# A two-layer hybrid decoder step: gate weights in 48 columns, norm vectors by rows, and head 0's projections dealt out between the small tokens' blocks of w_in

## The chip, the core and the metric

The kernel runs on one core of a Trainium2 chip. Its time is the device time of one execution, the median of several runs in microseconds (us). The core has five engines that work side by side, each in its own fixed order: TensorE (PE, matrix products into PSUM), VectorE (DVE), ScalarE (ACT), GpSimd (POOL), and SyncE (SP), which here only issues DMA transfers between the device's memory (HBM) and on-chip memory (SBUF). An engine that waits for something holds up all that stands behind it on that engine.

## The reference

One inference step of two layers, each followed by a squared-ReLU MLP and a layer norm. The first layer is gated linear attention (GLA), the second differential attention over a paged cache; the change lies in the first. Its input is a prompt of 1024 tokens, 16 meta tokens ahead of it, and 8 decode sequences with one new token each, every one with a stored state per head. In float32:

```python
h = x @ w_in                                    # 1024 -> q, k (4 heads x 128), v, r (4 x 256), g_low (16)
q, k, v, r, g_low = jnp.split(h, ...)
lg = log_sigmoid(g_low @ w_gate + b_gate) / 16  # one log decay per token, head and key column
b = cumsum(lg)                                  # within a chunk
o = (q * exp(b)) @ state + sum_j(q_i * k_j * exp(b_i - b_j)) v_j
new_state = exp(b_last) * state + (k * exp(b_last - b)).T @ v
out = (rms_norm(o, g_norm) * silu(r)) @ w_out   # then residual, layer norm with ln_mix_g, ln_mix_b
```

The outputs are both token sets after the two layers, the final GLA state of the prompt, the updated states of the 8 decode sequences, and the new rows of the cache.

## The kernel before

Products over the prompt are made exact enough for float32 by three products of a rounded type: an operand is split into a high and a low part, and `mm3` (L194 to L197) issues high x high, low x high and high x low. Weights are loaded as `raw` (L180) and split by ScalarE (L182) and GpSimd (L183). The prompt is transposed by TensorE (L264) and split (L191, L192) into XH and XL, in two halves `c` of 512 tokens.

The first layer runs in these steps, as the code is written:

- The meta and decode tokens, 24 rows called the small tokens, are multiplied with all of `w_in`. That streams in blocks of 1 MB through two buffers `swt`: eight blocks for q, k and v (L223, matmuls L280) and four for r (L229, L285).
- Their gate, scores and output follow in a chain across TensorE, ScalarE and VectorE: g_low (L324), transposes of q and k (L329), the gate product (L338), the transposed keys (L368), the meta tokens' state (L376, copied by ScalarE at L377), the scores (L385, L394), the product with v (L405).
- The 8 decode states, 512 KB each, pass through three buffers: load (L410), product (L413), the new k v term on GpSimd (L414), update on VectorE (L416), store (L417). The load of sequence `b + 3` waits for the store of sequence `b`.
- g_low of the prompt for both halves (L560), 16 columns of the array wide, three products for each of 8 blocks of the inner dimension.
- For each of four heads: q and k of both halves (matmuls at L195 to L197, 96 in all, copied to `gq` and `gk`, two buffers each), v of both halves (192 matmuls). Then for each half the gate product (L602), `log_gate` (ScalarE L314 to L316, VectorE L318 and L319), the running sum (L607), scores by a hierarchy of levels (VectorE L351, L356, L357; TensorE L617, L632), a transpose (L652), and outputs and state (L660 to L662).

PSUM is handed out by three pools: three banks `mmt` for the large products, three `axt` for transposes, gate products, scores and outputs, and `smt` for the small tokens.

The order on each engine is not that of the code. A scheduler places the instructions in a simulated timeline, by the order of the code as priority and by when operands and buffers are free; so work of head 1 can stand between steps of head 0. On SyncE a transfer also waits until an earlier one of its semaphore has landed.

## Time and profile before

| | us |
|---|---|
| median of 3 runs (lowest, highest) | 2921.35 (2921.29, 2924.93) |
| the profiled execution | 2915.81 |
| its span | 2914.1 |
| TensorE busy in the span | 2783.9 (96%) |
| VectorE, GpSimd, ScalarE busy | 1857.9, 1145.4, 1038.3 |
| mean granted TensorE clock | 0.978 |
| start of head 1's first gate product (L602) | 188.54 |

The page gives each engine's busy time over the whole span, an average over stages that are limited by different things. For a change in the first layer it is better to look at stretches of time there, at the waits of TensorE with what ended each, and at the rows of the engine that it waited for. The granted clock is the share of full speed that TensorE had. "L413 x24" counts records: a float32 product that isn't split leaves two.

### The profile page before, as it was taken

To read this page: it belongs to the slowest core of one execution; us is meant where nothing else is said; L and a number is where in the kernel's file an instruction comes from. 1 tells how busy PE (TensorE), PEld (TensorE's weight loads), DVE (VectorE), ACT (ScalarE), POOL (GpSimd) and SP (SyncE) were. 2 spreads that over 40 slices of the span, in tenths; PEclk is the share of its full clock that TensorE was granted. 3 is DMA by queue.
4 is the path that set the end of the run, shared out by engine and by line. 5 is a ranking of instruction groups with operands and counts; after the bars stand their busy time and mean duration, and the time that the engine had idled before them with its cause. 6 is when DMAs were issued, how large, how long until landed. Compare 5 with 4: busy or idle time off the path is not lost. (4 is left out here: it accounts for less than half of the span.)

```text
span 2914.1 us, 52192 instructions
## 1 busy us (share of the span) xinstructions
PE 2783.9 (96%) x19668; PEld 2275.1 (78%) x19668; DVE 1857.9 (64%) x2976; ACT 1038.3 (36%) x2071; POOL 1145.4 (39%) x885
## 2 busy tenths in 40 slices
PE   8999999999999999999989999989898999999996
PEld 5776668987777777777888986878788889797985
DVE  2664544458877877777676731878438755838378
ACT  2343354151122122122411111777325535345343
POOL 1321122234333333433323430122326766677666
PEclk9999999999999999999999998999899999999998
DMA  8667541524798888988488988463427878796972
GB/s 262 210 214 248 187 168 39 191 73 164 255 341 309 309 328 310 331 315 321 137 274 288 360 298 260 102 135 84 116 98 214 230 224 234 195 288 163 270 205 86
DMA packets 299308, 643.83 MB, mean 221 GB/s; under 512 B 35168, under 2 KB 150880, under 8 KB 287792
## 3 DMA queue, kind: packets, MB, share of 16 engines
q1 hardware_dynamic: 267520, 531.15, 52.8%
q0 software_dynamic: 31536, 109.35, 15.2%
q8 instruction: 155, 2.54, 0.3%
q14 instruction: 97, 0.79, 0.1%
HBM read 582.89 MB, written 40.91 MB: 214 GB/s over the span
## 5 line engine op out<-in xcount | busy, mean ns | idle before, releaser
L183 POOL TENSOR_TENSOR wlo<-raw,whi 128x512 fp32r<-128x512 f32 x256 | 361.2, 1425 | 786.0 <-ACT whi L182 697.6
L195 PE MATMUL mmt<-whi,XH 128*128 128x256 f32 (+1 forms) x1824 | 554.0, 305 | 7.5 <-DVE qr L1051 3.8
L196 PE MATMUL mmt<-wlo,XH 128*128 128x256 f32 (+1 forms) x1824 | 550.8, 303 | 0.5 <-POOL wlo L183 0.5
L195 PE MATMUL mmt<-XH,whi 128*128 128x512 f32 (+1 forms) x1376 | 480.1, 350 | 15.7 <-DVE HL L192 6.4
L197 PE MATMUL mmt<-XH,wlo 128*128 128x512 f32 (+1 forms) x1376 | 479.4, 350 | 0.0
L197 PE MATMUL mmt<-whi,XL 128*128 128x256 f32 x1536 | 440.5, 287 | 6.8 <-DVE XL L192 6.8
L195 PEld LDWEIGHTS mmt<-whi,XH 128*128 128x128 f32 x1824 | 346.3, 190 | 43.6 <-issue 19.8
L182 ACT CAST whi<-raw 128x512 fp32r<-128x512 f32 x256 | 152.4, 619 | 619.0 <-PE mmt L197 247.3
L196 PEld LDWEIGHTS mmt<-wlo,XH 128*128 128x128 f32 x1824 | 346.6, 190 | 25.0 <-issue 11.7
L771 DVE TENSOR_REDUCE sc<-pg 128x16 f32<-128x1024 f32 x256 | 309.6, 1214 | 78.4 <-POOL pg L770 74.9
L197 PEld LDWEIGHTS mmt<-whi,XL 128*128 128x128 f32 x1536 | 292.3, 190 | 22.7 <-issue 14.8
L196 PE MATMUL mmt<-XL,whi 128*128 128x512 f32 x768 | 307.6, 400 | 0.0
L195 PEld LDWEIGHTS mmt<-XH,whi 128*128 128x128 f32 x1376 | 261.2, 190 | 57.5 <-DVE HL L192 8.2
L770 DVE TENSOR_TENSOR pg<-pg,qb 128x1024 f32<-128x1024 f32 x192 | 261.3, 1366 | 59.1 <-DMA pg<-in_cache_k 42.9
L197 PEld LDWEIGHTS mmt<-XH,wlo 128*128 128x128 f32 x1376 | 261.2, 190 | 43.6 <-issue 12.0
L770 POOL TENSOR_TENSOR pg<-pg,qb 128x1024 f32<-128x1024 f32 x64 | 156.3, 2443 | 286.3 <-DMA pg<-in_cache_k 215.0
L195 PE MATMUL mmt<-whi,HH 128*128 128x512 f32 x512 | 205.3, 401 | 1.4 <-DVE Y L995 1.4
L196 PE MATMUL mmt<-wlo,HH 128*128 128x512 f32 x512 | 204.5, 399 | 0.0
L197 PE MATMUL mmt<-whi,HL 128*128 128x512 f32 x512 | 203.7, 398 | 0.0
L196 PEld LDWEIGHTS mmt<-XL,whi 128*128 128x128 f32 x768 | 145.2, 189 | 40.4 <-issue 8.9
L196 PE MATMUL mmt<-XH,whi 128*128 128x258 f32 x608 | 173.0, 286 | 3.7 <-DMA XH<-xc 2.9
L1397 POOL TENSOR_TENSOR wlo<-RW,whi 128x512 fp32r<-128x512 f32 x96 | 152.4, 1678 | 56.6 <-ACT whi L1396 56.5
(432 smaller groups left out, 5482.1 us busy)
## 6 DMA issues: line engine op xcount, KB each, us to landing
pg<-in_cache_k SPq DMA_DIRECT2D x256, 512.0 KB
pg<-in_cache_v SPq DMA_DIRECT2D x256, 512.0 KB
XH<-xc POOLq DMA_DIRECT2D x42, 1032.0 KB, 8.8
raw<-in_mlp_w SPq DMA_DIRECT2D x164, 256.0 KB
rw<-in_mlp_w SPq DMA_DIRECT2D x156, 256.0 KB
swt<-in_mlp_w SPq DMA_DIRECT2D x32, 1024.0 KB
RW<-in_mlp_w POOLq DMA_DIRECT2D x96, 256.0 KB, 7.3
xc<-XH POOLq DMA_DIRECT2D x14, 1032.0 KB, 8.0
```

The lines of the kernel that those rows point to most:

```text
L182: S.copy(hi[:, c], raw)
L183: G.tensor_tensor(lo[:, c], raw, hi[:, c].bitcast(F32), op=ALU.subtract)
L195: TE.matmul(ps, ah, bh, start=first, stop=False)
L196: TE.matmul(ps, ah, bl, start=False, stop=False)
L197: TE.matmul(ps, al, bh, start=False, stop=last)
L770: eng.tensor_tensor(pg, pg, qb, op=ALU.mult)
L771: return V.tensor_reduce(sc[:, n, :], pg.rearrange("p (h d) -> p h d", d=64), op=ALU.add, axis=AX.X).ins
L1397: G.tensor_tensor(lo[:, k, :], t, hi[:, k, :].bitcast(F32), op=ALU.subtract)
```

## The change

Five things change, all in the first layer.

1. The gate's weights stand in one tile `gw` of 48 columns: the high part in columns 0 to 15, zeros in 16 to 31, the low part in 32 to 47. One matmul with XH and one with XL for each block give both parts' products in different partitions; a copy and an add put them together. 32 matmuls stand where 48 stood.
2. The layer-norm vectors, the gate's bias and the GLA norm are loaded as rows of 128 elements (six transfers) into one tile and transposed by TensorE; four copies put them in place. Before, these were ten transfers of single 4-byte elements.
3. The q, k and v projections of a head are a generator `proj`. For head 0 one of its 8 tiles is emitted after the gate, and one after each second block of `w_in` or each block for r. The small tokens' chain so comes after head 0's projections in the code's order. The weights for v of head 0 are loaded earlier.
4. The loads of the decode states are not issued before the last block of `w_in`.
5. Both halves' gate products stand at a head's start, and hold two of the three `axt` banks.

```diff
@@ -226,9 +226,10 @@
     def sload2(w, k, eng=None):
 
         t = swt()
-        dma(t, w[k * P : (k + 2) * P, :].rearrange("(k p) n -> p k n", p=P))
+        swl.append(dma(t, w[k * P : (k + 2) * P, :].rearrange("(k p) n -> p k n", p=P)).ins)
         return t
 
+    swl = []
     sx = gp.tile([P, NB, TS], F32, name="sx")
     masks = gp.tile([P, 5, TS], U8, name="masks")
     Ats = [gp.tile([P, 4, P], F32, name="At%d" % i) for i in range(2)]
@@ -257,6 +258,9 @@
     qku = qk_unit(0)
     for t in range(4, 8):
         dma(Yt[:, t, :], A["x_prompt"][0, t * P : (t + 1) * P, :])
+    v0u = kunit(wi, 1024)
+    graw = gp.tile([P, NB, 16], F32, name="graw")
+    dma(graw, wir[:, :, 3072:3088])
     for c in range(2):
         for k in range(NB):
             ps = axt()
@@ -268,9 +272,72 @@
     mf = s4()[:, : 5 * TS]
     dma(mf, A["cm"].rearrange("p l t -> p (l t)"))
     V.tensor_copy(masks.rearrange("p l t -> p (l t)"), mf)
-    graw = gp.tile([P, NB, 16], F32, name="graw")
-    dma(graw, wir[:, :, 3072:3088])
     diag = cload("diag", gp)
+
+    prow = s2()[:, :P]
+    for i, nm in enumerate(("ln_mix", "ln_mlp")):
+        for j, gb in enumerate("gb"):
+            dma(prow[32 * i + 16 * j : 32 * i + 16 * j + 16, :], A[f"{nm}_{gb}"].rearrange("l (k p) -> (l k) p", p=P))
+    dma(prow[64:68, :], A["gla_b_gate"].rearrange("l (h p) -> (l h) p", p=P))
+    dma(prow[68:70, :], A["gla_norm"].rearrange("l (m p) -> (l m) p", p=P))
+    ps = smt()
+    TE.transpose(ps[:, :70], prow[:70, :], ident[:70, :70])
+    for i in range(2):
+        V.tensor_copy(lnp[:, i::2].rearrange("p l j k -> p j l k"), ps[:, 32 * i : 32 * i + 32].rearrange("p (j l k) -> p j l k", j=2, l=2))
+    bg = gp.tile([P, GH], F32, name="bg")
+    V.tensor_copy(bg, ps[:, 64:68])
+    gn = gp.tile([P, 2], F32, name="gn")
+    V.tensor_copy(gn, ps[:, 68:70])
+
+
+    def proj(h, qk):
+        hi, lo = qku if h == 0 else qk_unit(h)
+        hv, lv = (w.rearrange("p (i k n) -> p i k n", i=2, n=P) for w in (hi, lo))
+        for c in range(2):
+            cs = slice(512 * c, 512 * c + 512)
+            for i in range(2):
+                ps = mmt()
+                for k in range(NB):
+                    mm3(ps, hv[:, i, k, :], lv[:, i, k, :], XH[:, k, cs], XL[:, k, cs], k == 0, k == NB - 1)
+                t = g2.tile([P, 512], F32, name=("gq", "gk")[i])
+                if i == 0:
+                    S.activation(t, ps, AF.Copy, scale=P ** -0.5)
+                else:
+                    S.copy(t, ps)
+                qk[c, i] = t
+                yield
+        hi, lo = v0u if h == 0 else kunit(wi, 1024 + h * 256)
+        hv, lv = (w.rearrange("p (k n) -> p k n", n=256) for w in (hi, lo))
+        for c in range(2):
+            for i2 in range(2):
+                ps = mmt()
+                for i in range(2):
+                    t = 4 * c + 2 * i2 + i
+                    for k in range(NB):
+                        a = slice(t * P, (t + 1) * P)
+                        mm3(ps[:, i * 256 : (i + 1) * 256], XH[:, k, a], XL[:, k, a], hv[:, k, :], lv[:, k, :], k == 0, k == NB - 1)
+                S.copy(Yh[:, h, 4 * c + 2 * i2 : 4 * c + 2 * i2 + 2, :].rearrange("p i e -> p (i e)"), ps)
+                yield
+
+
+    gw = gp.tile([P, NB, 48], F32R, name="gw")
+    gz = s4()[:, : NB * 48].rearrange("p (k n) -> p k n", n=48)
+    V.memset(gz, 0.0)
+    V.tensor_copy(gz[:, :, :16], graw)
+    S.copy(gw, gz)
+    V.tensor_tensor(gw[:, :, 32:], graw, gw[:, :, :16].bitcast(F32), op=ALU.subtract)
+    gT = gp.tile([48, 512], F32, name="gT")
+    for c in range(2):
+        ps = mmt()
+        for k in range(NB):
+            for i, x in enumerate((XH, XL)):
+                TE.matmul(ps[:48, :], gw[:, k, :], x[:, k, 512 * c : 512 * c + 512], start=k + i == 0, stop=k + i == NB)
+        ga, gb_, go = ps[32 * c : 32 * c + 16, :], ps[32 - 32 * c : 48 - 32 * c, :], gT[32 * c : 32 * c + 16, :]
+        S.copy(go, gb_)
+        V.tensor_tensor(go, go, ga, op=ALU.add)
+    qk = {}
+    first = proj(0, qk)
+    next(first)
 
 
     pa, pb = smt(), smt()
@@ -278,11 +345,15 @@
         w = sload(wi[k * P : (k + 1) * P, 0:2048])
         for c in range(4):
             TE.matmul(pa[c * TS : (c + 1) * TS, :], sx[:, k, :], w[:, c * 512 : (c + 1) * 512], start=k == 0, stop=k == NB - 1)
+        if k % 2:
+            next(first)
     for k in range(0, NB, 2):
         w = sload2(wi[:, 2048:3072], k)
         for i in range(2):
             for c in range(GH):
                 TE.matmul(pb[c * TS : (c + 1) * TS, :256], sx[:, k + i, :], w[:, i, c * 256 : (c + 1) * 256], start=k + i == 0, stop=k + i == NB - 1)
+        next(first, None)
+    w_in = swl[-1]
     sqkv = s2()
     S.copy(sqkv, pa)
     sv = Y[:TS, 4096:5120]
@@ -298,15 +369,9 @@
 
     inv = cload("inv", gp)
     srope = cload("srope", gp)
-    for i, nm in enumerate(("ln_mix", "ln_mlp")):
-        for j, gb in enumerate("gb"):
-            for l in range(2):
-                dma(lnp[:, 2 * l + i, j, :], A[f"{nm}_{gb}"][l].rearrange("(k p) -> p k", p=P))
     wg = gp.tile([48, 512], F32, name="wg")
     for c in range(2):
         dma(wg[32 * c : 32 * c + 16, :], A["gla_w_gate"][0])
-    bg = gp.tile([P, GH], F32, name="bg")
-    dma(bg, A["gla_b_gate"][0].rearrange("(h p) -> p h", p=P))
 
     def log_gate(z, n, h):
 
@@ -407,7 +472,8 @@
     for b in range(NS):
         stt = Y[:, 5120 + 1024 * (b % 3) : 6144 + 1024 * (b % 3)].rearrange("p (h e) -> p h e", e=256)
         vb = vbs[:, b % 2, :].rearrange("p (h e) -> p h e", e=256)
-        dma(stt, A["state_gla"][0, b].rearrange("h d e -> d h e"))
+        with tc.issue_after(w_in):
+            dma(stt, A["state_gla"][0, b].rearrange("h d e -> d h e"))
         dma(vb.rearrange("p h e -> p (h e)"), A["vs"][b : b + 1, :].broadcast_to([P, D]))
         for h in range(GH):
             TE.matmul(po[h * TS : (h + 1) * TS, :256], qmk[:, h, b, :], stt[:, h, :], start=False, stop=b == NS - 1)
@@ -549,58 +615,20 @@
     dma(A["sxd"], sx)
 
 
-    ghi = gp.tile([P, NB, 16], F32R, name="ghi")
-    glo = gp.tile([P, NB, 16], F32R, name="glo")
-    split(ghi, glo, graw)
-    gT = gp.tile([48, 512], F32, name="gT")
-    for c in range(2):
-        cs = slice(512 * c, 512 * c + 512)
-        ps = mmt()
-        for k in range(NB):
-            mm3(ps[:16, :], ghi[:, k, :], glo[:, k, :], XH[:, k, cs], XL[:, k, cs], k == 0, k == NB - 1)
-        V.tensor_copy(gT[32 * c : 32 * c + 16, :], ps[:16, :])
-
-    gn = gp.tile([P, 2], F32, name="gn")
-    dma(gn, A["gla_norm"][0].rearrange("(m p) -> p m", p=P))
     gss = gp.tile([P, GH, 8], F32, name="gss")
 
     for h in range(GH):
-        hi, lo = qku if h == 0 else qk_unit(h)
-        hv, lv = (w.rearrange("p (i k n) -> p i k n", i=2, n=P) for w in (hi, lo))
-        qk = {}
+        if h:
+            for _ in proj(h, qk):
+                pass
+        st = SM[:, h, :]
+        pgs = [axt() for c in range(2)]
         for c in range(2):
+            TE.matmul(pgs[c], wg[32 * c : 32 * c + 16, h * P : (h + 1) * P], gT[32 * c : 32 * c + 16, :], start=True, stop=True)
+        for c in range(2):
+            q, k_, v = qk[c, 0], qk[c, 1], Yh[:, h, 4 * c : 4 * c + 4, :]
             cs = slice(512 * c, 512 * c + 512)
-            for i in range(2):
-                ps = mmt()
-                for k in range(NB):
-                    mm3(ps, hv[:, i, k, :], lv[:, i, k, :], XH[:, k, cs], XL[:, k, cs], k == 0, k == NB - 1)
-                t = g2.tile([P, 512], F32, name=("gq", "gk")[i])
-                if i == 0:
-                    S.activation(t, ps, AF.Copy, scale=P ** -0.5)
-                else:
-                    S.copy(t, ps)
-                qk[c, i] = t
-        hi, lo = kunit(wi, 1024 + h * 256)
-        hv, lv = (w.rearrange("p (k n) -> p k n", n=256) for w in (hi, lo))
-        vt = {}
-        for c in range(2):
-            v = Yh[:, h, 4 * c : 4 * c + 4, :]
-            for i2 in range(2):
-                ps = mmt()
-                for i in range(2):
-                    t = 4 * c + 2 * i2 + i
-                    for k in range(NB):
-                        a = slice(t * P, (t + 1) * P)
-                        mm3(ps[:, i * 256 : (i + 1) * 256], XH[:, k, a], XL[:, k, a], hv[:, k, :], lv[:, k, :], k == 0, k == NB - 1)
-                S.copy(v[:, 2 * i2 : 2 * i2 + 2, :].rearrange("p i e -> p (i e)"), ps)
-            vt[c] = v
-        st = SM[:, h, :]
-        for c in range(2):
-            q, k_, v = qk[c, 0], qk[c, 1], vt[c]
-            cs = slice(512 * c, 512 * c + 512)
-            ps = axt()
-            TE.matmul(ps, wg[32 * c : 32 * c + 16, h * P : (h + 1) * P], gT[32 * c : 32 * c + 16, :], start=True, stop=True)
-            m = log_gate(ps, 512, h)
+            m = log_gate(pgs[c], 512, h)
             b = g2.tile([P, 512], F32, name="gb")
             for i in range(4):
                 a = slice(i * P, (i + 1) * P)
```

In the places shown below, names are those of the tiles, with buffer numbers, and line numbers are of each kernel's own code. After the change L347 is the product of `w_in`'s blocks (L280 before), L389 g_low of the small tokens (L324), L459 and L470 the scores and the product with v (L394, L405), L479 and L482 the states' product and update (L413, L416), L627 the gate product (L602), L645 and L660 the score blocks (L617, L632), L383 and L384 the last steps of `log_gate` (L318, L319), and L416, L421 and L422 the levels (L351, L356, L357).

SyncE, the first transfers, before:

```order
L304 DMA lnp<-in_ln_mlp_b 128x8x1 x2
L307 DMA wg<-in_gla_w_gate 16x512 x2
L309 DMA bg<-in_gla_b_gate 128x4x1
L564 DMA gn<-in_gla_norm 128x2x1
L946 DMA ht<-in_ln_mix_g 128x256
L223 DMA swt<-in_gla_w_in 128x2048
L180 DMA raw<-in_gla_w_in 128x2x256
L223 DMA swt<-in_gla_w_in 128x2048
L180 DMA raw<-in_gla_w_in 128x2x256
L410 DMA Y<-in_state_gla 128x4x256 x3
```

SyncE, from the row transfers on, after:

```order
L280 DMA s_294<-in_ln_mix_b 16x128
L280 DMA s_294<-in_ln_mlp_g 16x128
L280 DMA s_294<-in_ln_mlp_b 16x128
L281 DMA s_294<-in_gla_b_gate 4x128
L273 DMA s_289<-in_cm 128x160
L282 DMA s_294<-in_gla_norm 2x128
L223 DMA swt<-in_gla_w_in 128x2048
L180 DMA raw<-in_gla_w_in 128x4x128
L223 DMA swt<-in_gla_w_in 128x2048
L147 DMA c_inv<-in_cf 128x128
L180 DMA raw<-in_gla_w_in 128x4x128
```

Before, two blocks of `w_in` (`swt`) go out ahead of the vectors and the third behind them; after, the first goes out behind the row transfers and the next ones soon after. The first three states stand behind the fourth block before, and after the last block now.

TensorE, the end of the small tokens' chain, before:

```order
L394 MATMUL smt<-t_520 32x32 x4
L196 MATMUL mmt<-wlo,XH_84 128x256
L197 MATMUL mmt<-whi,XL_86 128x256
L602 MATMUL axt<-gT,wg 128x512
L617 MATMUL axt<-gq,gk 32x32 x13
L405 MATMUL smt<-Y,sA 32x256 x4
L413 MATMUL smt<-Y,s_534 32x256 x12
L617 MATMUL axt<-gq,gk 32x32 x3
L195 MATMUL mmt<-XH_83,whi 128x512
L196 MATMUL mmt<-XL_85,whi 128x512
```

and after:

```order
L459 MATMUL smt<-t_860 32x32 x4
L459 MATMUL smt<-t_872 32x32 x4
L459 MATMUL smt<-t_884 32x32 x4
L459 MATMUL smt<-t_896 32x32 x4
L470 MATMUL smt<-Y,sA 32x256 x4
L479 MATMUL smt<-Y,s_910 32x256 x12
L660 MATMUL axt<-t_1470 32x64 x8
L660 MATMUL axt<-t_1486 32x32 x8
L645 MATMUL axt<-t_1503 32x32 x16
L645 MATMUL axt<-t_1527 32x32 x16
L645 MATMUL axt<-t_1551 32x32 x16
L479 MATMUL smt<-Y,s_910 32x256 x8
```

Before, v of head 0 (`mmt<-wlo,XH`) stands between the scores' steps, and q and k of head 1 (`mmt<-XH,whi`) follow the states' first products, 58 of them ahead of the first L632. After, the steps follow one another from the meta tokens' state to the score blocks of head 0. The 72 matmuls of head 1's q and k that can be run ahead stand further up: 21 between L394 (the transposes) and L403, 41 between L403 and L433, 10 between L433 and L441. At the start of TensorE's order, all 64 transposes of the prompt and the first block of `w_in` stand ahead of the first gate matmul, where before gate, q and k matmuls stood between the last 20 transposes.

VectorE, the first half of head 0, before:

```order
L395 COPY_PREDICATED sA<-masks,smt 16x4x16 x4
L318 TENSOR_SCALAR t_1450<-axt,bg 128x512
L416 SCALAR_TENSOR_TENSOR Y<-Y,ses,swt 128x256 x8
L620 TENSOR_TENSOR gAd<-axt,c_diag 128x128
L319 TENSOR_TENSOR t_1450<-t_1450,t_1446 128x512
L607 SCALAR_TENSOR_TENSOR gb<-ones,t_1450 128x128 x4
L351 TENSOR_TENSOR t_1477<-gb 128x512
L351 TENSOR_TENSOR t_1493<-gb 128x512
L351 TENSOR_TENSOR t_1510<-gb 128x512
L351 TENSOR_TENSOR t_1534<-gb 128x512
```

and after:

```order
L383 TENSOR_SCALAR t_1443<-axt,bg 128x512
L460 COPY_PREDICATED sA<-masks,smt 16x4x16 x3
L384 TENSOR_TENSOR t_1443<-t_1443,t_1439 128x512
L635 SCALAR_TENSOR_TENSOR gb<-ones,t_1443 128x128 x4
L416 TENSOR_TENSOR t_1470<-gb 128x512
L416 TENSOR_TENSOR t_1486<-gb 128x512
L416 TENSOR_TENSOR t_1503<-gb 128x512
L416 TENSOR_TENSOR t_1527<-gb 128x512
L416 TENSOR_TENSOR t_1551<-gb 128x512
L482 SCALAR_TENSOR_TENSOR Y<-Y,ses,swt 128x256 x4
L421 TENSOR_TENSOR t_1470<-t_1470,gk 128x4x64
L482 SCALAR_TENSOR_TENSOR Y<-Y,ses,swt 128x256 x4
```

Before, eight updates (two sequences) stand ahead of L319; after, the updates begin only behind the five steps of the levels.

## The prediction

> **What bounds the kernel now.** I read the page first: span, busy times.
>
> ```profile
> span 2914.1 us, 52192 instructions
> PE 2783.9 (96%) x19668; PEld 2275.1 (78%) x19668; DVE 1857.9 (64%) x2976; ACT 1038.3 (36%) x2071; POOL 1145.4 (39%) x885
> ```
>
> TensorE is busy for 96% of the span, so time is won by fewer matmul rows, by fewer waits of TensorE, or by a higher granted clock, and it is lost by new waits. The sum below is made against the profiled execution's 2915.81 us (span 2914.1), which is 5.5 us under the median of 2921.35; I carry the difference to the median. A change of 0.2%, 5.8 us, is about what a measurement of this kernel can tell from none.
>
> Next the busy time of each engine by stretches (columns: length, then each engine's busy time and instruction count, granted TensorE clock, mean share of the DMA engines, GB/s):
>
> ```profile
> 18.70:40.00 21.30, 16.45 (x91) 8.49 (x91) 5.77 (x10) 4.94 (x11) 2.54 (x2) 0.99 0.84 196
> 20.00:30.00 10.00, 10.00 (x59) 5.87 (x58) 3.82 (x8) 2.81 (x5) 1.46 (x2) 1.00 0.85 127
> 39.00:44.00 5.00, 5.00 (x19) 1.55 (x20) 1.28 (x2) 1.72 (x3) 1.65 (x2) 0.66 1.05 375
> 40.00:108.00 68.00, 68.00 (x544) 49.27 (x540) 15.03 (x49) 20.00 (x50) 16.39 (x12) 0.98 0.64 219
> 108.00:150.00 42.00, 37.97 (x379) 29.40 (x373) 36.22 (x70) 12.54 (x33) 18.22 (x11) 0.92 0.80 243
> 125.00:130.00 5.00, 5.00 (x124) 3.68 (x124) 5.00 (x14) 1.90 (x6) 0.00 (x0) 0.66 0.78 216
> 135.00:140.00 5.00, 5.00 (x26) 3.95 (x16) 3.52 (x10) 0.59 (x1) 1.90 (x1) 0.66 0.80 241
> 188.50:470.00 281.50, 267.75 (x2751) 192.23 (x2751) 137.24 (x297) 117.77 (x290) 57.56 (x34) 1.00 0.54 187
> ```
>
> The reader should see three things. From 40 to 108 us TensorE never idles. Before that it loses 21.30 − 16.45 = 4.85 us, after that 42.00 − 37.97 = 4.03. And after each of the longer waits there is a stretch of slow clock: at 0.66 over 5 us, 0.34 × 5 = 1.7 us of full-speed work is lost each time, three times. Where the time goes before 150 us, row by row on TensorE (start, busy time, line, operands; in brackets the wait ahead and what ended it):
>
> ```profile
> 22.24 0.40 PE L195 MATMUL mmt<-XH,whi 128*128 128x512 f32 x1
> 22.47 0.39 PE L196 MATMUL mmt<-XL,whi 128*128 128x512 f32 x1
> 23.87 1.48 PE L264 MATMUL axt<-c_ident,Y 128*128 128x128 f32 x12
> 34.26 0.40 PE L197 MATMUL mmt<-XH,glo 128*16 128x512 f32 x1
> 34.50 0.39 PE L195 MATMUL mmt<-XH,ghi 128*16 128x512 f32 x1
> 38.98 1.19 PE L280 MATMUL smt<-swt,sx 128*32 128x512 f32 x8 [4.09 <-DMA swt<-in_gla_w_in]
> 102.92 0.28 PE L196 MATMUL mmt<-wlo,XH 128*128 128x256 f32 x1
> 103.03 0.28 PE L197 MATMUL mmt<-whi,XL 128*128 128x256 f32 x1
> 104.52 1.12 PE L602 MATMUL axt<-gT,wg 16*128 16x512 f32 x2
> 105.94 0.63 PE L405 MATMUL smt<-Y,sA 32*32 32x256 f32 x8
> 106.50 1.50 PE L413 MATMUL smt<-Y,s 128*32 128x256 f32 x24
> 121.62 0.53 PE L632 MATMUL axt<-t 128*32 128x64 f32 x12
> 122.82 0.64 PE L413 MATMUL smt<-Y,s 128*32 128x256 f32 x8 [0.67 <-DMA Y<-in_state_gla]
> 124.93 0.53 PE L413 MATMUL smt<-Y,s 128*32 128x256 f32 x4 [1.20 <-DMA Y<-in_state_gla]
> 133.85 0.64 PE L413 MATMUL smt<-Y,s 128*32 128x256 f32 x8 [2.08 <-DMA Y<-in_state_gla]
> ```
>
> The waits are one for a block of `w_in` (L280) and three for decode states (L413, sequences 3, 4 and 5). Nothing waits between L602 and L632 because head 1's q and k matmuls (L195–L197) stand there.
>
> **The change, part by part.** The gate columns (g_low): 48 matmuls of 16 columns become 32 of 48. Start to start they take 34.50 − 34.26 = 0.24 us with 16 columns and 22.47 − 22.24 = 0.23 with 128, so 48 columns cost no more, and 16 × 0.23 = 3.7 us of TensorE leave. What comes in (a zeroing, two copies and a subtraction for the weights, a copy and an add for each chunk) is off the path: VectorE has 21.30 − 5.77 us free in the stretch from 18.7 to 40, and the result is read only by the gate product, which stands behind V of head 0. At the worst the weights' copies delay the first gate matmul by under 1 us.
>
> Norm vectors, and the wait at L280. Rows of SyncE's queue (start, time of issue):
>
> ```profile
> 17.35 2.37 SPq L269 DMA_DIRECT2D s<-in_cm  x1
> 24.76 2.95 SPq L304 DMA_DIRECT2D lnp<-in_ln_mlp_g  x2
> 27.75 1.46 SPq L304 DMA_DIRECT2D lnp<-in_ln_mlp_b  x2
> 31.96 0.38 SPq L223 DMA_DIRECT2D swt<-in_gla_w_in  x1
> 34.16 5.57 SPq L410 DMA_DIRECT2D Y<-in_state_gla  x3
> ```
>
> The third block of `w_in` is issued at 31.96, behind the small transfers that the order of SyncE shows, and is used at 38.98, 7.0 us later. In the stretch 20 to 30 us the DMA engines are 0.85 busy and move 127 GB/s, against 375 at a share of 1.05 from 39 to 44: the vectors fetched in 4-byte elements take the engines' time. After, these are rows of 512 bytes; the block and its neighbours go out ahead of the states, and the wait of 4.09 goes, with its slow stretch of 1.7. [...] What comes late next is the first block: it now stands behind seven small transfers, about where `cm` stands (17.35). With the same 7.0 us it arrives at 24.4. In the new order TensorE must have it ahead of the first gate matmul, and from 18.7 on has only 12 transposes (1.5 us) before it: a wait of up to 4.2 us, and none if it comes by 20.2. I take the middle, 2.5, since the vectors' elements no longer share the engines; the rest of the old loss there was 4.85 − 4.09 = 0.76, so +1.8 (bounds −0.8 and 3.4). The transposition of the vectors and its four copies are some 0.1 us on TensorE and under 1 us on an idle VectorE.
>
> So the front wins 3.7 + 4.1 + 1.7 − 1.8 = 7.7 us (bounds 6 and 10).
>
> The small tokens' chain (L324 to L413) moves behind the V matmuls of head 0. Nothing of it costs more TensorE time, but what covered its steps and the steps of head 0 after it is spent earlier. Head 1's q and k can run only 72 matmuls ahead, since three PSUM banks hold them while head 0 still has gq and gk; before, they stand behind L413, and 58 of them (13.3 us from 108.0 on) cover the time until L632. After, they stand between the steps L329, L338, L368 and L376 (21, 41 and 10 of them), and from L376 to the first L632 nothing else is there. Same work, new order: L413's first three sequences end before at 106.50 + 1.50 = 108.0; after, the 72 matmuls (16.6) and the second chunk's gate product (1.1) lie ahead of that, less 7.7: 118.0.
>
> What TensorE then waits for is read from VectorE and the queue of SyncE:
>
> ```profile
> 107.54 4.89 DVE L416 SCALAR_TENSOR_TENSOR Y<-Y,ses,swt 128x256 f32<-128x256 f32 x8
> 112.55 1.58 DVE L319 TENSOR_TENSOR t<-t,t 128x512 f32<-128x512 f32 x1
> 115.56 4.81 DVE L351 TENSOR_TENSOR t<-gb 128x512 f32<-128x512 f32 x5
> 123.68 1.66 DVE L416 SCALAR_TENSOR_TENSOR Y<-Y,ses,swt 128x256 f32<-128x256 f32 x4
> 128.53 1.28 DVE L351 TENSOR_TENSOR t<-gb 128x512 f32<-128x512 f32 x2
> 112.45 0.38 SPq L417 DMA_DIRECT2D out_gla_state_s<-Y  x1
> 114.75 0.58 SPq L410 DMA_DIRECT2D Y<-in_state_gla  x1
> 117.21 0.37 SPq L410 DMA_DIRECT2D Y<-in_state_gla  x1
> 125.37 0.38 SPq L417 DMA_DIRECT2D out_gla_state_s<-Y  x1
> 128.80 0.37 SPq L410 DMA_DIRECT2D Y<-in_state_gla  x1
> ```
>
> (a) Head 0's gate. L319 waited before for the updates (L416) and ran at 112.55. After, it waits for ScalarE, whose head-0 steps come behind the copies of L376's result and run beside L385, L394 and L405 on TensorE; if they end when L413 begins, 1.5 us ahead of 118.0, L319 stands at 116.5. From L319 to L632 it was 121.62 − 112.55 = 9.1; one update of 1.66 now stands between, and the five L351, 0.96 us each here, took 0.64 at 128.53. I keep 9.1: L632 at 125.6, a wait of 7.6 us (bounds 5 and 9).
>
> (b) The states. Buffers exist for three sequences; the load of sequence 3 must wait for the update and the store of sequence 0. Before, these updates ran from 107.54; after, they stand behind the five L351, which end 120.37 − 112.55 = 7.8 after L319, at 124.3. Two updates and a step between them: the second store leaves at 128.1. The loads followed the second store by 2.3 and 4.8 us (114.75 and 117.21 against 112.45), and their use followed by 8.1 and 7.7, in a later case by 5.1 (128.80 to 133.85). With 5.1, since less else is loaded at that time, sequences 3 and 4 come at 135.5 and 138. TensorE has little over 2 us of L632 and L617 work meanwhile (by 0.53 for the first twelve): a wait of about 8 us (bounds 4 and 14).
>
> (c) Sequences 5, 6 and 7: each needs an update, a store (3.4 us from 125.37 to 128.80) and a load (5.1), about 10 us a round with two in flight, and TensorE has some 12 us of work for the three, where the rounds take 17: 5 us (bounds 2 and 9).
>
> (d) The clock. I count two slow stretches of 1.7 in this part, 3.4 as before (bounds 0 and 5). [...]
>
> Together 7.6 + 8 + 5 + 3.4 = 24.0, where before had 0.67 + 1.20 + 2.08 + 3.4 = 7.4: 16.6 lost, less 7.7 won, is +8.9 us at the start of head 1.
>
> Heads 1 to 3: both chunks' gate products at a head's start let the second chunk's chain on VectorE begin earlier; the waits from 188.5 to 470 are 13.75 us in all, and part of them is VectorE's. I take −2 (bounds −5 and +5, since two of three axt banks are then held). The rest of the program is ordered alike up to layer 2's attention, where some matmuls change places: ±2, taken as 0. Sum: +6.9 us, 2922.7 for a profiled execution, 2928 at the median.
>
> **Rivals.** No change (2921): the waits (a) to (c) come out at their short ends, 5.5 + 4.5 + 2, because L351 takes 0.64 each (1.6 less in all) and the loads take 5.1 without fail. Then 15.4 − 7.4 − 7.7 − 2 = −1.7, within 0.2%. For it speak the two L351 of 0.64 and the one load of 5.1; against it that stores and loads of 512 KB stand in one another's way.
>
> Faster (2913): VectorE's chain of head 0 does not make TensorE wait, since head 0's gate is no longer behind eight updates (4.89 us). It decides if L632 starts by 119 and sequence 3 is there by 127; then only about 7 us are lost against 7.4, and −7.7 with −1 in the heads is kept: −8.4. Against it stands that L319 to L632 alone took 9.1.
>
> Slower still (2935): two axt banks held in every head stall L617, L632 and L660 by some 2 us a head, +7 on the forecast. For it speaks that these groups take turns on three banks; against it the early release, when VectorE reads the second product.
>
> The front does not do what it says (2934): the `w_in` blocks are paced by the transfers, not the queue. Twelve blocks of 1 MB at 375 GB/s are 2.8 us each, 34 in all, and the wait of 4.09 with its slow stretch comes back at another block: +5.8. Against it: 96 q and k matmuls at 0.23, 192 for V at 103.03 − 102.92 = 0.11 and the blocks' own twelve at 1.19 are 57 us of TensorE work beside them.
>
> **How the numbers follow.** The forecast (slower, 2921.35 + 6.9 = 2928, its own range 2927.2 to 2934) gets 0.34, the two slower rivals 0.16 together, no change 0.3, faster 0.2. So slower 0.5, same 0.3, faster 0.2. The range 2912 to 2940 reaches from the faster rival to the forecast with (b) and (c) near their upper bounds, and leaves out about 2 in 10.
>
> **What would show it.** Right: 32 gate matmuls, a wait of 2 to 3 us for the first block of `w_in` ahead of the gate and none over 2 us for a later one; L413's first sequences at 116 to 120; a wait for VectorE of 5 to 9 us ahead of L632 and one of 4 us or more for a state; head 1's gate product 5 to 13 us later than at 188.54. Wrong: TensorE busy from 118 to 126 (then 2913 to 2921), or a wait for `w_in` again before 90 us.

## The result, and the profile after

| | before | after |
|---|---|---|
| median of 15 runs each (us) | 2923.37 | 2936.11 |
| lowest to highest | 2911.84 to 2927.84 | 2915.67 to 2947.97 |
| profiled execution | 2915.81 | 2915.67 |

The ratio of after to before is 1.0036, with a 95% interval of 1.0020 to 1.0051, which leaves out 1: slower by about 10.5 us (the two medians are 12.7 apart). The runs of one kernel lie up to 1.1% apart, and both profiled executions stand near the lower end of theirs, so the two spans (2914.1 and 2913.8) say nothing of the difference. What they are good for is the order of events within the first layer.

The page of the changed kernel, and its stretches (length, busy time of TensorE, its weight loads, VectorE, ScalarE and GpSimd, granted clock, DMA share, GB/s):

```profile
span 2913.8 us, 52161 instructions
18.70:40.00 21.30, 19.34 (x98) 11.98 (x99) 8.41 (x19) 9.04 (x17) 7.71 (x6) 1.00 0.67 229
40.00:108.00 68.00, 68.00 (x497) 51.93 (x496) 9.53 (x27) 13.96 (x33) 14.07 (x10) 1.00 0.68 234
108.00:142.00 34.00, 22.37 (x315) 14.55 (x314) 29.64 (x72) 12.44 (x35) 6.01 (x3) 0.60 0.45 140
```

The last of these stretches in the kernel before, and two of its rows on TensorE (start, busy time, line):

```profile
108.00:142.00 34.00, 30.06 (x324) 22.54 (x317) 31.65 (x63) 9.67 (x25) 12.56 (x7) 0.90 0.83 248
188.54 1.12 PE L602 MATMUL axt<-gT,wg 16*128 16x512 f32 x2
649.43 0.39 PE L195 MATMUL mmt<-whi,HH 128*128 128x512 f32 x1
```

The front is better: from 18.7 to 40 us TensorE loses 21.30 − 19.34 = 1.96 us where before lost 4.85, at full clock. Then comes the loss: from 108 to 142 it is busy for 22.37 us of 34 at a clock of 0.60. In the kernel before, the same stretch had 30.06 at 0.90. Row by row on TensorE after the change (start, busy time, line, operands, wait and what ended it):

```profile
22.80 1.06 PE L347 MATMUL smt<-swt,sx 128*32 128x512 f32 x8 [0.55 <-DMA swt<-in_gla_w_in]
117.47 2.79 PE L479 MATMUL smt<-Y,s 128*32 128x256 f32 x24
125.43 1.49 PE L660 MATMUL axt<-t 128*32 128x64 f32 x32 [5.18 <-DVE t L422]
129.53 0.66 PE L645 MATMUL axt<-t 128*32 128x32 f32 x32 [1.32 <-DVE gAd L654]
132.93 1.08 PE L479 MATMUL smt<-Y,s 128*32 128x256 f32 x8 [2.74 <-DMA Y<-in_state_gla]
135.32 1.08 PE L479 MATMUL smt<-Y,s 128*32 128x256 f32 x8 [1.31 <-DMA Y<-in_state_gla]
148.77 0.64 PE L479 MATMUL smt<-Y,s 128*32 128x256 f32 x8 [1.90 <-DMA Y<-in_state_gla]
154.75 0.64 PE L479 MATMUL smt<-Y,s 128*32 128x256 f32 x8 [1.63 <-DMA Y<-in_state_gla]
161.20 0.70 PE L689 MATMUL axt<-gS,t 128*128 128x256 f32 x2 [2.89 <-DVE gS L692]
201.31 1.12 PE L627 MATMUL axt<-gT,wg 16*128 16x512 f32 x2
657.22 0.39 PE L195 MATMUL mmt<-whi,HH 128*128 128x512 f32 x1
```

The states' first products (L479, L413 before) stand at 117.47, and behind them follows a chain of waits for VectorE (L660, L645, L689) and for states. Head 1's first gate product (L627) comes at 201.31, 12.8 us later than the 188.54 of before. The last row is the first matmul of the MLP's first product, called the first up-projection below. Ahead of it TensorE has done the same work of layer 1 in all kernels, so it can be compared from one to the other: 657.22, against 649.43 before. What TensorE waited for, on VectorE and SyncE, after the change:

```profile
116.33 0.67 DVE L384 TENSOR_TENSOR t<-t,t 128x512 f32<-128x512 f32 x1
118.44 3.10 DVE L416 TENSOR_TENSOR t<-gb 128x512 f32<-128x512 f32 x5
121.46 1.67 DVE L482 SCALAR_TENSOR_TENSOR Y<-Y,ses,swt 128x256 f32<-128x256 f32 x4
125.07 0.38 SPq L483 DMA_DIRECT2D out_gla_state_s<-Y  x1
126.66 3.88 SPq L476 DMA_DIRECT2D Y<-in_state_gla  x2
```

The last step of head 0's gate (L384) begins at 116.33, the first state update (L482) comes behind the levels at 121.46, the second store at 125.07, and the loads of sequences 3 and 4 from 126.66. The gate is 3.8 us later than before (112.55); the first update (107.54), the second store (112.45) and the first of the two loads (114.75) are 12 to 14 us later.

### The profile page after: what moved, and what is told of

Read it like the earlier page. It is cut to its first block, busy times and chain, and to the rows that moved or that the text cites. A ratio compares the mean times of both kernels' runs of the same rounds, so it can differ in the third digit from the quotient of the medians.

```text
span 2913.8 us, 52161 instructions
## 1 busy us (share of the span) xinstructions
PE 2772.2 (95%) x19653; PEld 2269.7 (78%) x19653; DVE 1862.1 (64%) x2982; ACT 1042.5 (36%) x2075; POOL 1148.3 (39%) x885
```

## The experiments

Theory: the loss comes from the place of the small tokens' chain. It stands behind V of head 0, so that V no longer covers it, and what does cover it, head 1's q and k, is missing afterwards. Rivals: the state loads are issued too late; two held `axt` banks stall the heads; the front doesn't win what was forecast.

| kernel | median us | ratio to before (95%) | head 1's first gate product | first up-projection |
|---|---|---|---|---|
| before, two profiles | 2923 to 2929 | 1 | 188.5, 189.3 | 649.4, 655.2 |
| after, two profiles | 2936.1 | 1.0036 (1.0020, 1.0051) | 201.3, 202.2 | 657.2, 659.9 |
| no dealing, two profiles | 2908.4, 2908.1 | 0.9938 (0.9916, 0.9960), 0.9934 (0.9912, 0.9955) | 186.1, 185.9 | 645.0, 642.4 |
| q and k dealt | 2921.1 | 0.9976 (0.9960, 0.9993) | 184.6 | 650.8 |
| states early | 2936.5 | 1.0030 (1.0015, 1.0045) | 203.1 | 665.1 |
| gate in loop | 2936.9 | 1.0033 (1.0016, 1.0051) | 205.2 | 671.7 |
| front alone | 2928.6 | 1.0022 (1.0005, 1.0040) | 188.9 | 650.8 |
| no dealing, gate in loop | 2931.1 | 1.0008 (0.9990, 1.0026) | 188.5 | 658.3 |
| no dealing, states early | 2926.5 | 0.9999 (0.9980, 1.0019) | 184.6 | 645.9 |
| kept busy | 2924.0 | 0.9989 (0.9970, 1.0008) | 199.0 | 653.7 |
| kept busy, scores only | 2929.4 | 1.0009 (0.9994, 1.0023) | 200.7 | 657.9 |

The last two columns are from one profile each unless two are given. Two profiles of one kernel differ by up to 6 us at the first up-projection, and a profiled execution can lie far from its kernel's median: after's first 20 us below it, that of gate in loop 10 us above it. So differences of a few us in these columns carry little. The median of before moved between the sets of runs as well (2923.4 to 2929.3), so kernels are compared by their ratios.

What the scheduler did behind layer 1 matters for the times. Row by row in the traces, TensorE's order from the first up-projection on is that of before in three kernels: q and k dealt, and the two kept busy. The changed kernel and states early have another one within layer 2's attention, from 1804 us on. Gate in loop and the kernels without dealing differ from 1500 us or earlier as well, and front alone in three places near 1815 us. So a difference in time between two kernels can be put down to layer 1 only where this order is the same.

**No dealing.** The changed kernel without its third part's core:

```diff
-    next(first)
...
-        if k % 2:
-            next(first)
...
-        next(first, None)
...
-        if h:
-            for _ in proj(h, qk):
-                pass
+        for _ in proj(h, qk) if h else first:
+            pass
```

> All of the change except the dealing: none of head 0's projection tiles is emitted between the blocks of w_in, all stand behind the small tokens' chain in the code, so the scheduler puts the chain's steps between the V matmuls of head 0 again (gate in 48 columns, vectors by rows, late state loads and both gate products at a head's start stay). If the loss comes from the chain standing behind V, with head 1's q and k spent early: the waits of TensorE between 108 and 160 us fall from some 18 us to about 7, the long slow-clock stretch goes, head 1's first gate product comes at 181 to 186 us (201.3 in the changed kernel, 188.5 before), and the time is 5 to 10 us under before. If the loss comes from the late state loads or the held axt banks: head 1's first gate product stays at 197 or later and the time is some 10 us over before.

Its stretch from 108 to 142, and its waits of over a microsecond from 100 to 190 us (in all, times, longest):

```profile
108.00:142.00 34.00, 30.38 (x364) 22.66 (x363) 25.25 (x54) 9.22 (x21) 11.96 (x7) 0.90 0.76 239
...
PE smt L475 <- DMA Y<-in_state_gla: 3.6, 1, 3.6
PE axt L684 <- DVE gS L687: 3.3, 1, 3.3
PE axt L640 <- issue: 1.3, 1, 1.3
```

TensorE is busy for 30.38 us instead of 22.37, at 0.90 instead of 0.60; no wait for VectorE's levels of head 0 is left. Head 1's gate product stands at 186.1, 15.2 us earlier than in the changed kernel, at the late end of what the theory gave. The time is 17 to 21 us under before, more than the 5 to 10 expected. Repeated with other runs of before beside it:

> The kernel without dealing once more, timed in another set of runs, since it was the fastest (2908.4, ratio 0.9938). If that is the kernel's own, the ratio is 0.992 to 0.997 again and the profile has head 1's first gate product within 2 us of 186.1 and the first up-projection within 3 us of 645.0. If it was the runs' luck, the ratio is above 0.997.

0.9934, with both points of the profile again. So the kernel with the other four parts is 0.6% faster than before, and with the dealing added it is 0.4% slower. This is the fastest kernel of all. Not all of its gain is layer 1's: at the first up-projection it is 4 to 13 us ahead of before's two profiles, and the rest lies behind, where TensorE's order differs too.

**Q and k dealt.** The dealing is kept for q and k and dropped for v:

```diff
-        if k % 2:
+        if k % 2 and k < 7:
             next(first)
...
-        next(first, None)
...
-        if h:
-            for _ in proj(h, qk):
...
+        for _ in proj(h, qk) if h else first:
...
```

> The changed kernel, but only head 0's q and k tiles are dealt out between the blocks of w_in; its v tiles stand behind the small tokens' chain in the code, so v's matmuls can fill that chain. TensorE's order behind layer 1 is that of before, word for word. If the chain's place behind V is the cause of the loss, it goes here as it did without any dealing: no wait over 3 us for VectorE ahead of L632, head 1's first gate product at 181 to 190 us, the first up-projection 4 us or more ahead of before's 649.4, and a time 4 to 18 us under before. If dealing as such is the cause (projections between the blocks holding up the blocks): head 1's first gate product at 195 or later, and the time not under before. If the gain without dealing came from another order in the MLP and the attention, the time here is within 4 us of before, though head 1 starts early.

0.9976: the loss is gone, no wait for VectorE's score blocks from 100 to 190 us is longer than 0.9 us, and the clock from 108 to 142 is 0.95:

```profile
108.00:142.00 34.00, 30.86 (x371) 23.62 (x368) 26.69 (x55) 10.26 (x23) 11.83 (x7) 0.95 0.66 207
```

The blocks of `w_in` bear the projections between them. What the kernel doesn't bear is that v goes there too, since v is what the chain has to stand beside: head 1's first gate product is at 184.6 with v behind and at 201.3 with v dealt out. As TensorE's order behind layer 1 is that of before here, the gain of 0.24% can be put down to layer 1. The expected lead at the first up-projection is not there in its one profile (650.8, between the two of before), which was taken in an execution 7 us above the kernel's median.

**States early, and gate in loop.** Each undoes one other part of the changed kernel:

```diff
-        with tc.issue_after(w_in):
-            dma(stt, A["state_gla"][0, b].rearrange("h d e -> d h e"))
+        dma(stt, A["state_gla"][0, b].rearrange("h d e -> d h e"))
```

> The changed kernel, with only the rule gone that the first state loads wait for the last block of w_in; they stand behind the third block again. If the late loads are the cause: head 1's first gate product comes 5 us or more earlier than 201.3 and the time falls to within 4 us of before. If the chain's place is the cause: sequences 0 to 2 were there in time anyway, sequence 3 still waits for VectorE's updates, and nothing changes beyond 2 us: 201 again, and some 10 us over before; a wait for a w_in block of up to 4 us may come back.

```diff
-        pgs = [axt() for c in range(2)]
-        for c in range(2):
-            TE.matmul(pgs[c], wg[32 * c : 32 * c + 16, h * P : (h + 1) * P], ...)
...
-            m = log_gate(pgs[c], 512, h)
+            ps = axt()
+            TE.matmul(ps, wg[32 * c : 32 * c + 16, h * P : (h + 1) * P], ...)
+            m = log_gate(ps, 512, h)
```

> The changed kernel with the gate product of each half back in its half's loop, so that one axt bank is held instead of two. If held banks are the cause: 5 us or more less in heads 1 to 3 and the time within 4 us of before. If the chain's place is the cause: head 1's first gate product stays within 4 us of 201.3, and the time stays 6 to 14 us over before; the second half's chain starts later, so heads 1 to 3 lose some 2 to 4 us against the changed kernel.

Neither helps (1.0030 and 1.0033): head 1's first gate product is at 203.1 and 205.2. Both rivals fall. Without the early second product, the way from head 1's start to the first up-projection takes 671.7 − 205.2 = 466.5 us; with it, it took 455.9 and 457.7 in the changed kernel's two profiles. So the held banks are no visible cost, and perhaps a gain of some 10 us; the median doesn't show it, and q and k dealt, which has both products at the start too, takes 466.2.

**Front alone.** The kernel before with parts 1 and 2 only; the gate's weights and matmuls, as in the change, stand ahead of the blocks of `w_in`:

```diff
     diag = cload("diag", gp)
+    prow = s2()[:, :P]
+    for i, nm in enumerate(("ln_mix", "ln_mlp")):
+        for j, gb in enumerate("gb"):
+            dma(prow[32 * i + 16 * j : 32 * i + 16 * j + 16, :], ...)
...
+    gw = gp.tile([P, NB, 48], F32R, name="gw")
...
-    split(ghi, glo, graw)
-    gT = gp.tile([48, 512], F32, name="gT")
```

> The kernel before with the first two parts alone: gate weights in 48 columns, placed ahead of the blocks of w_in, and norm vectors by rows. No dealing, no late state loads, gate products in the loop. If the front wins what the prediction's sum says: the wait of 4.1 us for a block of w_in and its slow stretch go, 16 matmuls less, head 1's first gate product comes 6 to 9 us earlier than 188.5, and the time is 5 to 10 us under before. If transfers pace the front, the wait comes back at another block and the time is within 4 us of before.

Neither expectation holds as a whole. In the front the wait for a later block of `w_in` is down to 0.2 us, 0.69 us for the first one is left, and the stretch from 18.7 to 40 loses 2.2 us instead of 4.85. At the states' first products the lead is there:

```profile
110.92 1.50 PE L438 MATMUL smt<-Y,s 128*32 128x256 f32 x24
```

Ahead of this row stand 45 of head 1's q and k matmuls, where before has none ahead of its own at 106.50: 45 × 0.23 = 10.4 us more work, in 4.4 us more time, so 6 us ahead. But the time is 1.0022, slower than before. Head 1's first gate product does not come earlier either, and at the first up-projection the kernel stands at 650.8, between before's two. A part of the lead is given back between 108 us and head 1's gate product: TensorE idles there for 9.6 us, in before's two profiles for 4.7 and 7.3. So the front wins what was forecast where it stands, and nothing of it is left at the end of layer 1; the whole way of the loss is not settled.

**No dealing with one more part undone.** The two edits of states early and gate in loop, each made to the kernel without dealing.

> Without dealing, and with each half's gate product back in its loop. If both products at a head's start are worth something (in the dealt kernel heads 1 to 3 lost some 10 us without it, by the distance from head 1's first gate product to the first up-projection), the time is 4 to 10 us above the kernel without dealing (2908), head 1's start within 3 us of 186, and the rest lost from there to the first up-projection (645.0). If it is worth nothing, both stand within 3 us of that kernel.

> Without dealing, and with the state loads no longer bound to the last block of w_in. If the late loads help the front (the blocks of w_in come without the states beside them): a wait for a block of w_in of up to 4 us is back before 60 us and the time is 2 to 6 us above the kernel without dealing. If they do nothing: within 3 us of it, head 1's start at 186 as there.

With the gate product back in its loop the time goes from 2908 to 2931, and the first up-projection from 645.0 and 642.4 to 658.3: in these profiles both products at a head's start are worth 13 to 16 us within layer 1, more than the 4 to 10 expected. The rest of the 23 us lies behind it, where the order differs. With early state loads the time rises by 18 us, far more than the 2 to 6 expected, but the first up-projection, at 645.9, shows at most 3.5 of it, and the expected wait ahead of 60 us is not there: from 40 to 108 TensorE is busy for 67.52 of 68 us. The rest lies behind layer 1, where the scheduler's order on TensorE and SyncE differs between these two kernels as well, in the MLP and the attention. That part of the 0.6% can't be put down by these runs to what the edits do within layer 1.

**Kept busy.** Is the slow clock a cost of its own, or only a companion of waits? 70 matmuls that add nothing are put into the changed kernel; 20 of them are between the small tokens' scores, 50 behind the states' first products:

```diff
+    def warm(ps, n):
+        for _ in range(n):
+            TE.matmul(ps[:, 256:], XH[:, 0, 0:P], XH[:, 0, 0:256], start=True, stop=True)
...
+    warm(ps, 8)
...
+        if s in (4, 1):
+            warm(ps, 6)
...
+                if h == 0 and c == 0 and s == 64:
+                    with tc.issue_after(third):
+                        warm(ps, 30)
+                if h == 0 and c == 0 and s in (16, 4):
+                    warm(ps, 10)
```

> The changed kernel with 70 matmuls of 128 x 256 that add nothing (their results land in unused PSUM columns and are never read): 20 between the small tokens' scores, 30 behind the states' first products, 20 ahead of two of head 0's score levels, so that TensorE has large matmuls where it had only small ones and waits. This parts the slow clock from the waits. In the changed kernel the clock is at half from 114.7 to 142.0. If the slow stretch is a cost of its own: the clock from 108 to 142 is 0.9 or more, the states' first products take 1.5 us instead of 2.8, and head 1's first gate product comes 3 to 7 us earlier than 201.3 although 2.4 us of work are added ahead of the states (and the rest stands in waits). If the waits alone cost: the clock is full and head 1's first gate product comes at 201 to 204 all the same.

The second kernel has only the 20:

> As the kernel with 70 idle matmuls, but only the 20 between the small tokens' scores; the 50 behind the states' first products and ahead of head 0's score levels are gone. The scheduler again puts 18 of head 1's q and k matmuls ahead of sequences 3 and 4, where the changed kernel has none. If the gain of the 70 (2924 against 2936) came from this place of q and k, it is here as well: head 1's first gate product at 199 or earlier, and a ratio of 0.997 to 1.001. If it came from the clock: the wait behind the states' first products brings the slow clock as in the changed kernel (0.7 or less from 116 to 142), head 1's first gate product comes at 201 or later and the ratio is 1.002 or more.

The stretches 108 to 142, of the 70 and then of the 20, with the states' first products in each:

```profile
108.00:142.00 34.00, 27.70 (x341) 20.83 (x340) 25.99 (x68) 11.88 (x35) 4.09 (x2) 0.82 0.38 123
...
121.42 2.79 PE L486 MATMUL smt<-Y,s 128*32 128x256 f32 x24
```

```profile
108.00:142.00 34.00, 24.47 (x353) 18.36 (x352) 25.30 (x67) 12.52 (x35) 4.22 (x2) 0.85 0.35 110
...
122.11 1.50 PE L486 MATMUL smt<-Y,s 128*32 128x256 f32 x24
```

With 70 matmuls more the kernel is faster than the changed one (ratio 0.9989 against 1.0036), and head 1's start is 2.3 us earlier, although they are some 8 us of work (70 at the 0.12 by which v's matmuls of that shape stand apart). So TensorE had room for 8 us of anything in there. A cost of the clock of its own is borne out by half: 0.82 instead of 0.9 or more, the states' first products still at 2.79, and head 1's start short of the 3 to 7 us. With the 20 alone the clock stays up as well (0.85) and the states' products take 1.50 us, but head 1's start gains under 1 us on the changed kernel's first profile and the first up-projection nothing; its ratio lies between (1.0009). Neither expectation of that run fits. In this profile, holding the clock up ahead of a wait was worth little by itself: behind the faster matmuls came longer waits for VectorE (4.71 and 1.51 us at head 0's score blocks). The full separation fails, since in both kernels the scheduler also moved 18 or 19 of head 1's q and k matmuls between the states' products.

The second of the two shows something else. Its layer 1 is as late as the changed kernel's (200.7 and 657.9 against 201.3 and 657.2), but its order behind layer 1 is that of before, and its ratio of 1.0009 can't be told from 1. By that, up to 8 of the changed kernel's 10.5 us come from the other order in the attention, and not from the delay in layer 1; the two intervals overlap, so the size is uncertain.

**After and before again.** A second profile of each.

> The changed kernel once more, for a second execution's profile. The first one was profiled at 2915.7, its runs have a median of 2936. If the excess of the usual execution lies in layer 1, head 1's first gate product and the first up-projection come later than 201.3 and 657.2 by most of it; if it lies in the clock of the later stages, these two stand within 3 us and the granted clock from 1450 us on is lower than in the first profile.

> The kernel before once more, for a second execution's profile: the first was profiled at 2915.8, 10 under the median of its later runs (2926 to 2929). If the excess of the usual execution lies in layer 2's attention and its clock, as it did for the changed kernel, the first up-projection comes within 3 us of 649.4 and the attention (1799.4 to 2110.4 in the first profile, 311 us) takes 5 us or more longer.

Layer 1 repeats: 202.2 against 201.3, and 189.3 against 188.5. At the first up-projection the changed kernel is 7.8 us behind in the first pair and 4.7 in the second. The executions differ behind it. Of after's 20 us between its two profiles, 2.7 stand at the first up-projection; layer 2's attention takes 304.5 us in the first and 318.7 in the second, with the clock from 1800 to 1850 us at 0.83 and 0.66:

```profile
1800.00:1850.00 50.00, 46.21 (x289) 40.37 (x289) 35.36 (x118) 30.75 (x73) 4.85 (x9) 0.83 0.48 105
```

```profile
1800.00:1850.00 50.00, 43.38 (x232) 35.48 (x230) 25.58 (x85) 23.72 (x54) 4.85 (x9) 0.66 0.56 128
```

For before neither half of the expectation holds: 311.0 and 314.9 us in the attention, 3.9 more instead of 5 or more, and 5.8 more at the first up-projection instead of under 3.

## Why the prediction was right

The forecast was slower, 2928 with a range of 2912 to 2940. Measured was a ratio of 1.0036, 2932 by the median that it started from. The sign and the range hold, and so does the mechanism at the start of head 1: the chain stands uncovered behind V, and TensorE waits for VectorE's levels and the states. The terms were sized differently, and two of the signs named did not come: the wait of 2 to 3 us for the first block of `w_in` (0.55), and a wait of 4 us or more for a state (2.74 at most).

- **The front** (7.7 us won). 32 gate matmuls stand 0.23 us apart and the wait at L280 is gone. From 18.7 us on TensorE waits for 1.96 us in all ahead of the gate, near the 2.5, but only 0.55 of them are for the block of `w_in`; the rest are for the vectors' rows (0.35, the end of a wait of 0.83) and for VectorE's split of the prompt (0.34 and 0.72). That the single elements held the transfers up is not shown apart from the rest of the order; measured from 18.7 to 40 us are 196 GB/s at a DMA share of 0.84 before, and 362 at 1.04 in front alone. The states' first products begin at 117.47 against 106.50 before, with 17.7 us more work ahead of them: 6.7 us ahead. Front alone had 6 at the same point.
- **The place of the chain** (first products' end at 118.0). They begin within 1 us of 116.5, and end at 120.26, 2.3 us late, of which 1.3 are from running at half clock: 2.79 us instead of 1.50.
- **(a) VectorE's levels** (L632 at 125.6 after a wait of 7.6). Measured 125.43, after 5.18; the late end of the first products filled the difference. L319 was forecast for 116.5 and began at 116.33.
- **(b) Sequences 3 and 4** (135.5 and 138, 8 us). Measured 132.93 and 135.32, with waits of 1.32, 2.74 and 1.31: 5.4 us. L351 took 0.62 each where the sum kept 0.96. The 8 us were added up short: from L632 at 125.6 to sequence 4 at 138 with little over 2 us of work, the prediction's own figures give about 10.
- **(c) Sequences 5 to 7** (5 us). Waits of 1.90 and 1.63, and one that the prediction did not have: 2.89 at L689, for the head's state on VectorE, which stood behind the updates. Together 6.4. The kernel without dealing has that last wait too (3.3 at its L684), so the dealing didn't bring it.
- **(d) The clock** (3.4 us, two stretches). This term was mis-sized. The clock stood at half from 114.7 to 142.0 without a break, 27.3 us, and TensorE was busy for 2.92 + 13.15 us of them, 8.0 us of full-speed work lost; with a shorter one near 164 it is 9.5. The prediction counted its stretches behind longer waits, as before had them; here the clock fell ahead of the first of these (5.18 us, until 125.43). The stretches after 114.7 overlapped the waits, so not all of it came on top.
- **Head 1** (+8.9, 5 to 13). Measured +12.8 and +12.9.
- **Heads 1 to 3** (−2). Measured −5.0 and −8.2 by the two pairs of profiles. The runs with the gate product back in its loop point to the cause: in these pairs both products at a head's start are worth 9 to 13 us from head 1's start to the first up-projection. The size is not settled, since over all profiles kernels with both at the start take 454.7 to 466.2 us for that way and kernels without 460.9 to 469.9. The prediction had the sign and a fraction of the size, and a rival that made it a loss.

That the sum came so near is luck in part. (a) to (d) measure 5.2, 5.4, 6.4 and 9.5, together 26.5 for the 24.0 of the sum, but (a) and (b) are 5 us smaller and (c) and (d) 7.5 larger, and (d) overlaps the others. The way from L319 to L632 came out at the 9.1 that was kept, though two updates stood in it where one was reckoned (1.67 more): other steps were shorter by as much (L319 took 0.67 instead of 1.58). And layer 1 as a whole, 7.8 and 4.7 us late for a forecast of 6.9, has head 1 later by 4 and heads 1 to 3 faster by 3 to 6 than was said.

By layer 1 alone the loss should be 5 to 8 us; measured are about 10.5. By that difference 3 to 6 us lie behind the first up-projection, and by the kernel kept busy for the scores up to 8. There the order on TensorE is changed in layer 2's attention, a term taken as 0 with ±2. No profile shows this part itself: behind the first up-projection the changed kernel is 8 us faster than before in the first pair and equal in the second. Two profiles of each kernel are too few to place it, and this part of the cause stays open.

Of the rivals, the faster one fell at its own point of decision: L632 at 125.43, not 119. Its reason was sound in part: the five L351 took 3.10 us instead of 4.81, but two updates of 1.67 stood between them and L632. Its sum has a slip: 7 − 7.4 − 7.7 − 1 is −9.1, not −8.4. No change had (a) and (b) nearer than the forecast (5.5 and 4.5), and fell by (c) and by the clock. Slower still by the held banks was refuted, and so was a front paced by the transfers.

## What to carry to other kernels

Work that fills is a store, and a change that moves it says when the store is empty: before dealing out one stage's matmuls earlier, ask which later chain of small steps they stood beside. Here q and k could go between the blocks of `w_in` and v could not, because v covered the small tokens' chain. And several parts that come in one change should be timed apart: the kernel with four of the five was 0.6% faster than before, and the fifth hid it. Where a scheduler orders the whole program, an edit in one layer can also change the order in another, so the order behind the edit has to be compared before a difference in time is put down to it.

## What the runs showed that I had not expected

The clock fell without an idle stretch. In the changed kernel TensorE's last matmul on the whole array ahead of the chain begins at 110.93. From 111.4 to 114.7 it is busy for 2.90 us of 3.30, but with matmuls of 32 rows or 32 columns, and then the clock halves (columns as above; the matmul rows give rows and columns of the array in use). In the changed kernel's second profile it does so at 115.2, at the same place in the chain:

```profile
110.93 0.40 PE L197 MATMUL mmt<-XH,wlo 128*128 128x512 f32 x1
111.25 1.99 PE L441 MATMUL smt<-Y,t 32*128 32x256 f32 x8
113.17 0.44 PE L450 MATMUL smt<-sqk 128*32 128x32 f32 x8
```

```profile
111.40:114.70 3.30, 2.90 (x32) 2.16 (x32) 0.71 (x5) 1.97 (x4) 0.00 (x0) 1.00 0.00 0
114.70:118.10 3.40, 2.92 (x32) 1.60 (x36) 2.85 (x9) 1.05 (x2) 0.00 (x0) 0.50 0.02 5
118.10:142.00 23.90, 13.15 (x242) 8.33 (x231) 23.70 (x49) 8.13 (x22) 6.01 (x3) 0.50 0.63 198
142.00:145.00 3.00, 3.00 (x20) 2.03 (x19) 2.17 (x6) 0.00 (x0) 0.19 (x1) 1.00 0.93 346
```

It came back at 142.0, 4.2 us after the first of a run of large matmuls (137.79). With 20 matmuls of 128 x 128 among the same small ones, the states' first products ran at full speed in one kernel, and not in the other, which had waited 2.1 us ahead of them just the same. Whether the fall goes with the small matmuls or with the short waits among them (0.37 us and less), the runs don't tell apart, since the 20 filled some of these waits too.
